# A residual kept in DRAM by plain copies, its squares and norm moved into the up projection

## The chip, the cores and the metric

One Trainium2 chip, one of its NeuronCores. The time is the device time of one execution of the whole program in microseconds (us); the shown time is the median of three runs. All data are float32. Matrix products run with operands split into two float32r parts, a high and a low one, three products for one.

## The reference

One decoder layer on x of 512 tokens by 2048 features. Only the end of it is touched:

```python
x = x + concat([attn, ssm]) @ w_out                # second residual
x = x + cross_attention(rms_norm(x, g_cross), ...) # third residual, ends with @ w_co
hm = rms_norm(x, g_mlp)                            # needs the sum of squares of each token
x = x + square(relu(hm @ w_up)) @ w_down           # w_up 2048x8192, w_down 8192x2048
```

The factor of `rms_norm` for one token, 1/sqrt(mean(x*x) + eps), is one number per token. It can be multiplied onto `hm @ w_up` behind the product, which is what the kernel does.

## The kernel before

Activations are held transposed: features on the 128 partitions, 512 tokens along the row. The residual is thus 16 blocks of 128x512 (256 KB each). Almost all scratch blocks come from one pool of 68 buffers of 128x512, `big()`; a new block waits until every reader of the old one is done, transfers included.

The cross-attention section runs from line 988 and is written under `manual_schedule`: on each engine its instructions keep the order in which they are written. Behind it the planner orders the instructions by their order in the text and by when it takes them to be ready. Instructions of the up projection may fall between those of the section.

The output product of the cross attention (lines 1053 to 1075) makes four groups of four feature blocks, n = 0 to 3. For each block `third_out` adds the second residual (`xr`, read from DRAM by `load_cols` on GpSimd's queue) to the PSUM bank, on VectorE, and scales it by g_mlp on ScalarE. `forms` makes from two such blocks the seven sums and differences that a Strassen-like 2x2 scheme with seven products needs, split in high and low parts (`XF`, which stays in 56 of the 68 buffers for the whole up projection). `third_keep(n)` then stores what is still needed of the third residual: it squares the four blocks on ScalarE and adds the squares into four DRAM tiles (`ss3d`, accumulating transfers on GpSimd's queue, a plain write for n = 0), and writes the halves of the blocks as initial values into the DRAM accumulators `accd` of the down projection (four plain pieces and one accumulating piece for two blocks). `clear()` has written zeros into the other pieces of `accd` much earlier, in 24 small transfers.

The up projection makes 32 pairs of column blocks, f = 0 to 31. Each has four quarters; a quarter is 42 matmuls of 256 columns (`up_products`, lines 946 to 948) on one weight tile of 512 KB, which SyncE's queue loads (line 913) and `up_forms` turns into forms: lines 926 and 931 on ScalarE (`rh`, `wh`), lines 927 to 930 and 932 on VectorE (`sw`, `rl`, `wl`). Weight tiles have four raw buffers, forms two sets. The seven products lie in four PSUM banks, which `combine` (lines 952 to 962) turns into two result blocks, and `up_finish` multiplies them with the token factor `rb`, takes relu and square, and writes them to DRAM on ScalarE's queue. The banks alternate between two sets of four, `mm` and `aux`.

f = 0 is computed inside the section (lines 1077 to 1088), f = 1 behind it. At the end of f = 1 `third_norm` (lines 974 to 986) reads the four `ss3d` tiles back on SyncE's queue, adds them on VectorE, sums over features with eight matmuls with a column of ones (line 261), makes 1/sqrt with six small instructions that alternate between VectorE and ScalarE (lines 175 to 180), and spreads the result over the partitions by four transposes on TensorE (line 984). Then f = 0 and f = 1 can be finished.

Of the kernel before, what the change touches and what calls it, by code (L numbers as in the profile page):

```python
# [9 lines left out]
F32 = mybir.dt.float32  # L10
F32R = mybir.dt.float32r
I32 = mybir.dt.int32
AF = mybir.ActivationFunctionType
OP = mybir.AluOpType
# [3 lines left out]
D = 2048  # L18
NT = 4
NK = 16  # L20
# [85 lines left out]
def tile_layer(ctx, tc, vec, xT, memT_d, pos, wqk, wv0, wv1, wv2, wzx, wout, wcq, wckv, wco, wup, wdn, out):  # L106
    nc = tc.nc
# [25 lines left out]
    def big(dtype=F32):  # L133
        return bp.tile([128, 512], dtype, name="b", tag="b")
# [4 lines left out]
    def small(w, name="s"):  # L139
        return sp.tile([128, w], F32, name=name, tag=f"s{w}", bufs=4 if w > 32 else 12)  # L140
# [31 lines left out]
    def rsqrt(dst, ssq, n):  # L172
        w = ssq.shape[1]
        v, y, t = small(w, "v"), small(w, "y"), small(w, "t")
        dve.tensor_scalar(v, ssq, 1.0 / n, EPS, op0=OP.mult, op1=OP.add)
        act.activation(y, v, AF.Ln)
        act.activation(y, y, AF.Exp, scale=-0.5)
        dve.tensor_tensor(t, y, y, OP.mult)
        dve.scalar_tensor_tensor(t, t, -0.5, v, op0=OP.mult, op1=OP.mult)
        dve.scalar_tensor_tensor(dst, t, 1.5, y, op0=OP.add, op1=OP.mult)  # L180
# [77 lines left out]
    def token_sums(sq, nt, tag="aux"):  # L258
        p, s = bank(tag), small(nt, "ts")
        for t in range(nt):  # L260
            pe.matmul(p[:, t:t + 1], sq[:, t * 128:t * 128 + 128], onec, start=True, stop=True)
        dve.tensor_copy(s, p[:, :nt])
        return s
# [605 lines left out]
    def third_out(n, xr, ps):  # L869
        xs = []  # L870
        for i in range(4):
            dve.tensor_tensor(xr[i], xr[i], ps[i], OP.add)
            xs.append(big())
            act.activation(xs[i], xr[i], AF.Copy, scale=c_mlp[:, 4 * n + i:4 * n + i + 1])
        return xs

    NJ = D // 256
    accd = [[dp.tile([128, 512 if b < 3 else 256], F32, name=f"acc{j}_{b}") for b in range(4)] for j in range(NJ)]  # L880
    ss3d = [dp.tile([128, 512], F32, name=f"ss{i}") for i in range(4)]

    def third_keep(n, xr):
        for i in range(4):
            q = big()
            act.activation(q, xr[i], AF.Square)
            if n:
                nc.gpsimd.dma_start(ss3d[i], q, accum_op=OP.add)
            else:
                nc.gpsimd.dma_start(ss3d[i], q)  # L890
        for i in range(2):
            xa, xb, b, m = xr[2 * i], xr[2 * i + 1], accd[2 * n + i], big()
            act.activation(m, xb, AF.Copy, scale=-1.0)
            nc.gpsimd.dma_start(b[1][:, H0], xa[:, H0])
            nc.gpsimd.dma_start(b[0][:, H1], xa[:, H1])
            nc.gpsimd.dma_start(b[3], m[:, H0])
            nc.gpsimd.dma_start(b[2][:, H1], m[:, H1])
            nc.gpsimd.dma_start(b[0][:, H1], xb[:, H1], accum_op=OP.add)

    def clear():  # L900
        z = big()
        nc.gpsimd.memset(z[:, H0], 0.0)
        for b in accd:
            for to in (b[0][:, H0], b[1][:, H1], b[2][:, H0]):
                nc.gpsimd.dma_start(to, z[:, H0])


    prods = ((4, 4, 0, H0), (5, 5, 1, H0), (6, 0, 3, H0), (2, 3, 2, H0), (3, 2, 2, H1), (1, 1, 1, H1), (0, 6, 0, H1))
# [2 lines left out]
    def up_weights(f, q, w=wup):  # L911
        raw = weight_tile["raw"]()
        nc.sync.dma_start(raw, w[f, q].rearrange("p a b c -> p (a b c)"))
        return raw
# [56 lines left out]
    def up_out(f, ps):  # L971
        up_finish(f, combine(ps, True))

    def third_norm():

        s4, r3 = [big() for _ in range(4)], small(4, "r3")
        for i in range(4):
            nc.sync.dma_start(s4[i], ss3d[i])
        for i in range(3):
            dve.tensor_tensor(s4[0], s4[0], s4[i + 1], OP.add)  # L980
        rsqrt(r3, token_sums(s4[0], NT, "mm"), D)
        p = bank("mm")
        for t in range(NT):
            pe.transpose(p[:, t * 128:t * 128 + 128], r3[:, t:t + 1].to_broadcast([128, 128]), ident)
        act.activation(rb[:, :512], p, AF.Copy)
        act.activation(rb[:, 512:], p[:, H0], AF.Copy)

    uw, uf = [], []
    with tc.manual_schedule():

        ps = [bank("mm") for _ in range(NT)]
        for k in range(8):
            take()
            mem_unit(k)
            take()
            if k == 4:
                rsqrt(r2, token_sums(acc2[0], NT), D)
            mms(ps, x2T, k, k, 8)

        psk = [bank() for _ in range(2)]  # L1000
        for k in range(8):
            take()
            if k == 0:
                dve.tensor_tensor(msq[0][:, H0], msq[0][:, H0], msq[0][:, H1], OP.add)
                qc = rows_out(ps, r2)
            if k == 1:
                sq = head_sums(qc)
            if k == 2:
                rq = head_rstd(sq)
            if k in (3, 4):  # L1010
                head_scale(qc, rq, (2 * k - 6, 2 * k - 5))
            if k == 5:
                mem_rstd()
            if k > 5:
                qcT += [head_T(qc, h, cqs) for h in (2 * k - 12, 2 * k - 11)]
            mms(psk, memT, 8 + k, k, 8)

        pend = []
        psv = [bank("mm") for _ in range(2)]
        for k in range(8):  # L1020
            take()
            if k == 0:
                kc = rows_out(psk, rm)
                sq = head_sums(kc)
            if k == 1:
                head_scale(kc, head_rstd(sq), range(2))
                xr = [load_cols(0)]
                clear()
            if k == 3:
                kcT += [head_T(kc, h, c_ck) for h in range(4)]  # L1030
            if k >= 4:
                for tp in range(2):
                    e = scores(k - 4, tp)
                    if pend:
                        normalize(*pend.pop())
                    pend.append(e)
            mms(psv, memT, 16 + k, k, 8)
        normalize(*pend.pop())
        vc = rows_out(psv, rm)
        pt = [probs_T(0), probs_T(1)]  # L1040
        OcT = []
        for h in range(4):
            OcT.append(weighted(h, pt[h], vc))
            if h < 2:
                pt.append(probs_T(h + 2))
        xr.append(load_cols(1))
        uw += [up_weights(0, 0), up_weights(0, 1), up_weights(0, 2)]

        def co(n, ps, k):
            for i in range(4):  # L1050
                mm3(ps[i], tuple(a[:, i * 128:i * 128 + 128] for a in cow[4 * n + k]), OcT[k], k == 0, k == 3)

        for n in range(4):
            ps = [bank("aux" if n % 2 else "mm") for _ in range(NT)]
            co(n, ps, 0)
            if n == 0:
                uf += [up_forms(w) for w in uw[:2]]
            if n in (1, 3):
                co(n, ps, 1)
            if n:  # L1060
                xc = xs
                hl = big(F32R), big(F32R)
                forms(xc[0], xc[1], hl, H0)
                third_keep(n - 1, xr[n - 1])
            if n in (1, 2):
                xr.append(load_cols(n + 1))
            if n in (0, 2):
                co(n, ps, 1)
            co(n, ps, 2)
            if n > 1:  # L1070
                forms(xc[2], xc[3], hl, H1)
            co(n, ps, 3)
            xs = third_out(n, xr[n], ps)
            if n == 1:
                forms(xc[2], xc[3], hl, H1)
        uw.append(up_weights(0, 3))
        pu = up_bank(0)
        up_products(pu, (0, 1), uf[0], XF, True, False)
        uf.append(up_forms(uw[2]))
        xc = xs  # L1080
        hl = big(F32R), big(F32R)
        forms(xc[0], xc[1], hl, H0)
        third_keep(3, xr[3])
        up_products(pu, (2, 3), uf[1], XF, False, False)
        uf.append(up_forms(uw[3]))
        forms(xc[2], xc[3], hl, H1)
        for q in (2, 3):
            up_products(pu, (2 * q, 2 * q + 1), uf[q], XF, False, q == 3)

    first_out = combine(pu, True)  # L1090


    NU = FF // 256

    def up_pairs(fs):
        for f in fs:
            ps = up_bank(f)
            for q in range(4):
                wf = up_forms(up_weights(f, q))
                up_products(ps, (2 * q, 2 * q + 1), wf, XF, q == 0, q == 3)  # L1100
            if f == 1:
                third_norm()
                up_finish(0, first_out)
            up_out(f, ps)

    up_pairs(range(1, NU - 4))

# [212 lines left out]
```

## Time and profile before

| | us |
|---|---|
| median of 3 runs (2328.46 to 2336.8) | 2331.66 |
| the profiled execution | 2326.44 |
| its span, first to last instruction | 2324.7 |
| TensorE busy | 2300.5 (99%) |
| VectorE busy | 1744.9 (75%) |
| ScalarE busy | 1186.8 (51%) |
| GpSimd busy | 203.9 (9%) |

Engines in the rows: PE is TensorE, PEld its weight loads, DVE VectorE, ACT ScalarE, POOL GpSimd, SP SyncE; a q behind the name is the engine's own queue. L888 is line 888. The granted clock (PEclk) is a share of full speed, 1.00 being 2.4 GHz and 0.50 being 1.2 GHz. Busy time is a union of intervals, so instructions that overlap by a pipeline's length count once. The cross-attention section's last part and the first pairs of the up projection lie between 970 and 1110 us of the span.

### The profile page before, as it was taken

How to read it: one execution, taken by the hardware profiler on the slowest of the kernel's cores; microseconds unless marked ns; L12 is line 12 of the kernel's file. 1: busy time of each engine (PE TensorE's matmuls, PEld its weight loads, DVE VectorE, ACT ScalarE, POOL GpSimd, SP SyncE). 2: the span in 40 equal slices, each digit the busy share in tenths (PEclk: the TensorE clock that was granted, in tenths of full speed). 3: DMA queues.
4: the chain of work that ended last, by engine and by line, in shares of the span. 5: the costliest groups of instructions: out<-in, count | busy, mean ns of one | idle time of the engine just before them, and what ended most of it. 6: DMA issues, size and time to landing. Idle time of an engine off the chain costs nothing.

```text
span 2324.7 us, 39884 instructions
## 1 busy us (share of the span) xinstructions
PE 2300.5 (99%) x15700; PEld 2107.1 (91%) x15700; DVE 1744.9 (75%) x2970; ACT 1186.8 (51%) x1845; POOL 203.9 (9%) x271
## 2 busy tenths in 40 slices
PE   9999999999999999999999999999999999999999
PEld 7889977777778888789999999999999999999999
DVE  7544277786674446688888888888998988888976
ACT  6335377655453336564444444444565555665653
POOL 0000000000000002150000000000032121332120
PEclk9999999999999999999999999999999999999999
DMA  5222311212224457384433334434597685987784
GB/s 201 86 93 76 103 64 55 64 64 82 74 74 156 140 180 255 124 195 153 136 128 132 128 132 137 133 131 136 164 245 186 170 204 161 225 206 181 220 213 171
DMA packets 129597, 335.74 MB, mean 144 GB/s; under 512 B 14848, under 2 KB 30336, under 8 KB 129408
## 3 DMA queue, kind: packets, MB, share of 16 engines
q1 hardware_dynamic: 82944, 256.61, 33.3%
q0 software_dynamic: 30848, 55.59, 13.1%
q10 hardware_dynamic: 15616, 20.98, 2.4%
q8 instruction: 123, 2.02, 0.3%
q14 instruction: 66, 0.54, 0.1%
HBM read 258.67 MB, written 74.45 MB: 143 GB/s over the span
## 4 chain that ended last, share of the span: by engine, by line
PE 92%; DMA 2%; DVE 2%; ACT 2%; issue 1%; POOL 1%; SPq 0%; DVEq 0%; POOLq 0%; ACTq 0%
PE mm L220 11%; PE mm L222 11%; PE mm L221 11%; PE mm L948 9%; PE mm L946 9%; PE mm L947 9%; PE aux L948 9%; PE aux L946 9%; PE aux L947 9%; DMA acc<-b 1%; PE aux L531 1%; PE aux L522 1%; PE aux L256 1%; PE aux L648 0%; PE aux L503 0%
## 5 line engine op out<-in xcount | busy, mean ns | idle before, releaser
L931 ACT ACTIVATE wh<-sw 128x1024 fp32r<-128x1024 f32 x253 | 268.1, 1060 | 380.1 <-PE mm L947 128.7
L932 DVE TENSOR_TENSOR wl<-sw,wh 128x1024 fp32r<-128x1024 f32 x253 | 308.8, 1221 | 124.9 <-ACT wh L931 124.5
L216 DVE TENSOR_TENSOR wl<-wr,wh 128x1024 fp32r<-128x1024 f32 (+2 forms) x143 | 166.6, 1165 | 193.9 <-ACT wh L215 193.3
L215 ACT ACTIVATE wh<-wr 128x1024 fp32r<-128x1024 f32 (+2 forms) x143 | 144.7, 1012 | 285.2 <-PE mm L222 151.4
L946 PE MATMUL mm<-b,wh 128*128 128x256 f32 x1024 | 288.8, 282 | 0.0
L948 PE MATMUL mm<-b,wl 128*128 128x256 f32 x1024 | 288.6, 282 | 0.0
L947 PE MATMUL mm<-b,wh 128*128 128x256 f32 x1024 | 287.7, 281 | 0.0
L946 PE MATMUL aux<-b,wh 128*128 128x256 f32 x1000 | 281.5, 282 | 0.0
L948 PE MATMUL aux<-b,wl 128*128 128x256 f32 x1000 | 281.0, 281 | 0.0
L947 PE MATMUL aux<-b,wh 128*128 128x256 f32 x1000 | 280.4, 280 | 0.0
L222 PE MATMUL mm<-b,wl 128*128 128x512 f32 x640 | 254.5, 398 | 1.1 <-DVE wl L216 1.1
L221 PE MATMUL mm<-b,wh 128*128 128x512 f32 x640 | 255.2, 399 | 0.0
L220 PE MATMUL mm<-b,wh 128*128 128x512 f32 x640 | 254.9, 399 | 0.1
L926 ACT ACTIVATE rh<-wr 128x768 fp32r<-128x768 f32 x190 | 161.4, 849 | 151.4 <-PE aux L947 56.7
L1193 POOL DMA_DIRECT2D acc<-b x160 | 139.8, 1324 | 1063.1 <-ACT b L1192 1062.0
L946 PE MATMUL mm<-b,rh 128*128 128x256 f32 x768 | 219.2, 285 | 4.7 <-ACT rh L926 4.3
L948 PE MATMUL mm<-b,rl 128*128 128x256 f32 x768 | 218.7, 285 | 1.0 <-DVE rl L930 1.0
L947 PE MATMUL mm<-b,rh 128*128 128x256 f32 x768 | 218.5, 285 | 0.0
L946 PE MATMUL aux<-b,rh 128*128 128x256 f32 x750 | 213.0, 284 | 0.0
L947 PE MATMUL aux<-b,rh 128*128 128x256 f32 x750 | 212.7, 284 | 0.0
L948 PE MATMUL aux<-b,rl 128*128 128x256 f32 x750 | 212.3, 284 | 0.0
L220 PE MATMUL mm<-wh,b 128*128 128x512 f32 (+2 forms) x544 | 201.6, 371 | 2.8 <-ACT b L430 1.6
(324 smaller groups left out, 5846.8 us busy)
## 6 DMA issues: line engine op xcount, KB each, us to landing
wr<-in_wup_dram SPq DMA_DIRECT2D x96, 512.0 KB, 3.4
wr<-in_wdn_dram SPq DMA_DIRECT2D x96, 512.0 KB, 4.6
acc<-b POOLq DMA_DIRECT2D x120, 256.0 KB, 6.6
wr<-in_wzx_dram SPq DMA_DIRECT2D x48, 512.0 KB, 3.3
zr<-in_wup_dram SPq DMA_DIRECT2D x32, 512.0 KB, 3.2
a<-b ACTq DMA_DIRECT2D x64, 256.0 KB, 2.2
b<-a SPq DMA_DIRECT2D x64, 256.0 KB, 5.7
zr<-in_wdn_dram SPq DMA_DIRECT2D x32, 512.0 KB, 3.9
```

What stands on the lines that cost most here:

```text
L215: act.activation(hi, raw, AF.Copy)
L216: dve.tensor_tensor(lo, raw, hi.bitcast(F32), OP.subtract)
L220: pe.matmul(ps, l[0], r[0], start=start, stop=False)
L221: pe.matmul(ps, l[0], r[1], start=False, stop=False)
L222: pe.matmul(ps, l[1], r[0], start=False, stop=stop)
L926: act.activation(rhi, q(raw, 0, 3), AF.Copy)
L931: act.activation(shi, sw, AF.Copy)
L932: dve.tensor_tensor(slo, sw, shi.bitcast(F32), OP.subtract)
L946: pe.matmul(ps[b][:, H], w[0][:, d], xf[0], start=st, stop=False, skip_group_check=True)
L947: pe.matmul(ps[b][:, H], w[0][:, d], xf[1], start=False, stop=False, skip_group_check=True)
L948: pe.matmul(ps[b][:, H], w[1][:, d], xf[0], start=False, stop=sp_, skip_group_check=True)
L1193: nc.gpsimd.dma_start(accd[j][b], o[:, w], accum_op=OP.add)
```

## The change

`third_out` writes each finished block of the third residual to a DRAM tile `x3d` by a plain transfer on ScalarE's queue. The squares and the initial values of the accumulators are no longer made in the section. In f = 1 and f = 2 of the up projection two blocks per quarter are read back on SyncE's queue, squared on ScalarE and added up on VectorE (`third_sum`). `third_norm` is split: the sum over features and the 1/sqrt come behind the first quarter of f = 3, the transposes (`third_rows`) behind its third, and there f = 0, 1 and 2, whose combined results are held till then, are finished. The calls of `third_keep` and `clear` in the section are gone; the five transfers of the old `third_keep` are those of the new one. In f = 4 to 11 one pair of blocks each is read back again, and `third_keep` writes its pieces, and the zeros of that pair, on GpSimd's queue.

```diff
             xs.append(big())
             act.activation(xs[i], xr[i], AF.Copy, scale=c_mlp[:, 4 * n + i:4 * n + i + 1])
+            act.dma_start(x3d[4 * n + i], xr[i])
         return xs
...
-    ss3d = [dp.tile([128, 512], F32, name=f"ss{i}") for i in range(4)]
-
-    def third_keep(n, xr):
-        for i in range(4):
-            q = big()
-            act.activation(q, xr[i], AF.Square)
-            if n:
-                nc.gpsimd.dma_start(ss3d[i], q, accum_op=OP.add)
-            else:
-                nc.gpsimd.dma_start(ss3d[i], q)
-        for i in range(2):
-            xa, xb, b, m = xr[2 * i], xr[2 * i + 1], accd[2 * n + i], big()
-            act.activation(m, xb, AF.Copy, scale=-1.0)
-            (five transfers on GpSimd's queue, as below)
-
-    def clear():
+    x3d = dp.tile([NK, 128, 512], F32, name="x3d")
+
+    def third_block(i):
+        b = big()
+        nc.sync.dma_start(b, x3d[i])
+        return b
+
+    def third_keep(j):
+        xa, xb, b, m = third_block(2 * j), third_block(2 * j + 1), accd[j], big()
+        act.activation(m, xb, AF.Copy, scale=-1.0)
+        nc.gpsimd.dma_start(b[1][:, H0], xa[:, H0])
+        nc.gpsimd.dma_start(b[0][:, H1], xa[:, H1])
+        nc.gpsimd.dma_start(b[3], m[:, H0])
+        nc.gpsimd.dma_start(b[2][:, H1], m[:, H1])
+        nc.gpsimd.dma_start(b[0][:, H1], xb[:, H1], accum_op=OP.add)
         z = big()
         nc.gpsimd.memset(z[:, H0], 0.0)
-        for b in accd:
-            for to in (b[0][:, H0], b[1][:, H1], b[2][:, H0]):
-                nc.gpsimd.dma_start(to, z[:, H0])
+        for to in (b[0][:, H0], b[1][:, H1], b[2][:, H0]):
+            nc.gpsimd.dma_start(to, z[:, H0])
+
+    acc3 = []
+
+    def third_sum(i):
+        b = third_block(i)
+        act.activation(b, b, AF.Square)
+        if i:
+            dve.tensor_tensor(acc3[0], acc3[0], b, OP.add)
+        else:
+            acc3.append(b)
...
+    r3 = cp.tile([128, 4], F32, name="r3")
+
     def third_norm():
-        s4, r3 = [big() for _ in range(4)], small(4, "r3")
-        for i in range(4):
-            nc.sync.dma_start(s4[i], ss3d[i])
-        for i in range(3):
-            dve.tensor_tensor(s4[0], s4[0], s4[i + 1], OP.add)
-        rsqrt(r3, token_sums(s4[0], NT, "mm"), D)
+        rsqrt(r3, token_sums(acc3[0], NT, "mm"), D)
+
+    def third_rows():
         p = bank("mm")
         for t in range(NT):
             pe.transpose(p[:, t * 128:t * 128 + 128], r3[:, t:t + 1].to_broadcast([128, 128]), ident)
...
-    first_out = combine(pu, True)
     NU = FF // 256
+    held = [combine(pu, True)]
 
     def up_pairs(fs):
         for f in fs:
             ps = up_bank(f)
             for q in range(4):
                 wf = up_forms(up_weights(f, q))
+                if f in (1, 2):
+                    for i in range(2):
+                        third_sum(8 * f - 8 + 2 * q + i)
                 up_products(ps, (2 * q, 2 * q + 1), wf, XF, q == 0, q == 3)
-            if f == 1:
-                third_norm()
-                up_finish(0, first_out)
-            up_out(f, ps)
+                if f == 3 and q == 0:
+                    third_norm()
+                if f == 3 and q == 2:
+                    third_rows()
+                    for i in range(3):
+                        up_finish(i, held[i])
+                if 4 <= f < 4 + NJ and q == 1:
+                    third_keep(f - 4)
+            if f < 3:
+                held.append(combine(ps, True))
+            else:
+                up_out(f, ps)
```

## Rows read from the trace of the kernel before

**Rows 1.** The page: the whole span, busy us of each engine.
```profile
PE 2300.5 (99%) x15700; PEld 2107.1 (91%) x15700; DVE 1744.9 (75%) x2970; ACT 1186.8 (51%) x1845; POOL 203.9 (9%) x271
```
**Rows 2.** Windows: busy us by engine, then granted clock, DMA share, GB/s.
```profile
core 0: us, PE busy (x) PEld busy (x) DVE busy (x) ACT busy (x) POOL busy (x), PEclk, DMA share, GB/s
970.00:1010.88 40.88, 40.88 (x183) 33.84 (x181) 32.08 (x61) 28.43 (x51) 18.40 (x31) 1.00 0.57 151
1010.88:1060.81 49.93, 44.69 (x340) 43.45 (x338) 41.45 (x72) 26.93 (x42) 23.21 (x35) 0.93 0.84 216
1060.81:1090.55 29.74, 24.96 (x189) 24.87 (x189) 22.35 (x41) 12.52 (x18) 0.00 (x0) 0.89 0.38 125
1090.55:1110.55 20.00, 20.00 (x171) 20.00 (x170) 17.22 (x27) 8.96 (x12) 0.00 (x0) 1.00 0.41 134
```
**Rows 3.** Timeline of TensorE: start, us, instruction, idle before and releaser.
```profile
1010.88 0.28 PE L946 MATMUL mm<-b,rh 128*128 128x256 f32 x1
...
1022.36 0.38 PE L946 MATMUL mm<-b,rh 128*128 128x256 f32 x1 [1.32 <-ACT rh L926]
...
1032.84 0.39 PE L946 MATMUL mm<-b,rh 128*128 128x256 f32 x1 [2.94 <-ACT rh L926]
...
1060.61 0.95 PE L261 MATMUL mm<-onec,b 128*128 128x1 f32 x8
1066.34 1.12 PE L984 MATMUL mm<-cst,r 128*128 128x128 f32 x4 [4.78 <-DVE r L180]
...
1067.47 0.41 PE L947 MATMUL mm<-b,rh 128*128 128x256 f32 x1
```
**Rows 4.** Timeline of ScalarE in the second wait.
```profile
1030.51 0.63 ACT L893 ACTIVATE b<-b 128x512 f32<-128x512 f32 x1 [1.49 <-DMA acc<-b]
...
1031.96 0.83 ACT L926 ACTIVATE rh<-zr 128x768 fp32r<-128x768 f32 x1
```
**Rows 5.** Timeline of GpSimd: two transfers of the keeping, the last loads of xr.
```profile
1008.66 0.89 POOL L898 DMA_DIRECT2D acc<-b x1 [5.28 <-DVE b L712]
1013.59 2.52 POOL L866 DMA_DIRECT2D b<-x2d x4
```
**Rows 6.** Timeline of VectorE.
```profile
1016.08 0.69 DVE L195 TENSOR_TENSOR b<-b 128x512 fp32r<-128x512 f32 x1 [1.63 <-DMA acc<-b]
1017.68 2.00 DVE L872 TENSOR_TENSOR b<-b,aux 128x512 f32<-128x512 f32 x3 [0.90 <-DMA b<-x2d]
1024.66 0.42 DVE L852 TENSOR_TENSOR b<-b 128x256 f32<-128x256 f32 x1
1026.46 1.89 DVE L195 TENSOR_TENSOR b<-b 128x512 fp32r<-128x512 f32 x3
1054.21 0.69 DVE L980 TENSOR_TENSOR b<-b 128x512 f32<-128x512 f32 x1 [1.33 <-DMA b<-ss]
```
**Rows 7.** Page, DMA issues: count, KB each, median us to landing.
```profile
x2d<-b ACTq DMA_DIRECT2D x16, 256.0 KB, 2.0
ss<-b POOLq DMA_DIRECT2D x16, 256.0 KB, 7.5
b<-ss SPq DMA_DIRECT2D x4, 256.0 KB, 4.4
```
**Rows 8.** Groups of ScalarE, 975 to 1036 us: busy us, mean ns, idle before.
```profile
L886 ACT ACTIVATE b<-b 128x512 f32<-128x512 f32 x16 | 8.7, 616 | 0.0
L893 ACT ACTIVATE b<-b 128x512 f32<-128x512 f32 x8 | 4.7, 619 | 1.8 <-DMA acc<-b 1.8
```
**Rows 9.** ScalarE's queue, line 686: its 16 issues, ns min/median/max.
```profile
L686 ACTq DMA_DIRECT2D x2d<-b x16: 326/326/344, 708.2 to 856.7; - x16
```
**Rows 10.** Groups of VectorE, 1140 to 1300 us (eight pairs f).
```profile
L932 DVE TENSOR_TENSOR wl<-sw,wh 128x1024 fp32r<-128x1024 f32 x32 | 39.1, 1221 | 20.6 <-ACT wh L931 20.6
L967 DVE SCALAR_TENSOR_TENSOR b<-b,rb 128x512 f32<-128x512 f32 x16 | 10.3, 681 | 0.0
```
**Rows 11.** Waits of SyncE's queue, 1080 to 1300 us: total, times, longest.
```profile
SPq L913 <- DVE sw L929: 105.6, 22, 5.4
```

More of the change, by code (lines that the diff above doesn't have):

```diff
@@ L880, in tile_layer @@
     accd = [[dp.tile([128, 512 if b < 3 else 256], F32, name=f"acc{j}_{b}") for b in range(4)] for j in range(NJ)]
-    ss3d = [dp.tile([128, 512], F32, name=f"ss{i}") for i in range(4)]
-    def third_keep(n, xr):
-        for i in range(4):
-            q = big()
-            act.activation(q, xr[i], AF.Square)
-            if n:
-                nc.gpsimd.dma_start(ss3d[i], q, accum_op=OP.add)
-            else:
-                nc.gpsimd.dma_start(ss3d[i], q)
-        for i in range(2):
-            xa, xb, b, m = xr[2 * i], xr[2 * i + 1], accd[2 * n + i], big()
-            act.activation(m, xb, AF.Copy, scale=-1.0)
[L894 to L898, printed above, removed]
-    def clear():
+    x3d = dp.tile([NK, 128, 512], F32, name="x3d")
[11 more added lines that the diff above has]
+        nc.gpsimd.dma_start(b[0][:, H1], xb[:, H1], accum_op=OP.add)
         z = big()
         nc.gpsimd.memset(z[:, H0], 0.0)
-        for b in accd:
-            for to in (b[0][:, H0], b[1][:, H1], b[2][:, H0]):
-                nc.gpsimd.dma_start(to, z[:, H0])
+        for to in (b[0][:, H0], b[1][:, H1], b[2][:, H0]):
[8 more added lines that the diff above has]
+            acc3.append(b)
     prods = ((4, 4, 0, H0), (5, 5, 1, H0), (6, 0, 3, H0), (2, 3, 2, H0), (3, 2, 2, H1), (1, 1, 1, H1), (0, 6, 0, H1))
@@ L1027, in tile_layer @@
                 xr = [load_cols(0)]
-                clear()
             if k == 3:
@@ L1063, in tile_layer @@
                 forms(xc[0], xc[1], hl, H0)
-                third_keep(n - 1, xr[n - 1])
             if n in (1, 2):
@@ L1082, in tile_layer @@
         forms(xc[0], xc[1], hl, H0)
-        third_keep(3, xr[3])
         up_products(pu, (2, 3), uf[1], XF, False, False)
```

## The prediction

> **What bounds the kernel now.** I read the page's busy times first, then windows over the up projection, then TensorE's timeline and, back from each of its waits, the engine that ended it. The page shows TensorE busy for 99% of the span [rows 1]: only stretches where it waits, or runs at half clock, can be won. The windows say where. From 1090.55 on, one pair f takes 20.00 us with TensorE busy throughout at a granted clock of 1.00. The three pairs before it (f = 0 to 2) take 49.93 + 29.74 = 79.67 us where three such pairs take 60.00. The loss is 19.7 us, all of it beside the code that the change touches [rows 2]. In the stretch ahead, 970 to 1010.88, TensorE is busy for all 40.88 us [rows 2], so nothing can be won there.
>
> The loss has two halves. Between 1010.88 and 1060.81 it is 49.93 - 40.00 = 9.9 us: 5.2 us idle (49.93 - 44.69), the rest mostly half clock after the waits (mean granted clock 0.93) [rows 2]. The two longest waits are 1.32 and 2.94 us, both for ScalarE's `rh` [rows 3]. Behind the second stands a ScalarE that cannot go on: line 893, the negated copy of `third_keep`, waits 1.49 us for a buffer that a transfer into `accd` still reads, and `rh` is queued behind it [rows 4]. GpSimd's queue is late in the same way: its accumulating piece waits 5.28 us (for the plain piece that it adds to, by the code), and the loads of `xr` for n = 3 come out only at 1013.59, behind it [rows 5]. VectorE, in turn, waits for such a buffer (1.63 us) and for `xr` (0.90 us), and starts the last `third_out` at 1017.68, though TensorE had the banks ready by 1010.88 [rows 3, 6]. Between 1060.81 and 1090.55 the loss is 29.74 - 20.00 = 9.7 us [rows 2]: 4.78 us waiting for r3, then `rb`'s transposes, and matmuls at a duration of 0.41 instead of 0.28 us, at half clock [rows 3].
>
> **The change part by part.** All times stand against the profiled execution (2326.44 us, span 2324.7, so 1.7 us around it); it lies 5.2 us under the median shown, and I carry the difference over to that.
>
> (a) The section. ScalarE loses 16 squares and 8 copies, 8.7 + 4.7 = 13.4 us [rows 8], and gets 16 issues of 0.326 us [rows 9], 5.2 us. GpSimd's queue keeps only the loads of `xr`, so these are issued as soon as four buffers are free. The buffers of a block come free after one plain write, whose kin landed in 2.0 us, not after squares and a chain of accumulating transfers, which landed in 7.5 us [rows 7]. The Trainium skill ("DMA: Bandwidth & Descriptors", "Latency and other measured facts") gives about 0.6 us to the first byte of a transfer of SyncE's or ScalarE's queue and about 1 us for GpSimd's; going by those 0.4 us alone the buffers would hardly come sooner and (a) would keep nearly all of its 9.9 us. The rows disagree: 5.5 us apart, the accumulation and the queue ahead of it included.
>
> What is late next in f = 0 is VectorE. From 1010 on it owes four adds of `third_out`, two `up_forms` and two `forms`. The adds come at 2.00 us for three, 2.7 for four; one `forms` went from 1024.66 to 1028.35, 3.7 us [rows 6]; one `up_forms` is at most (17.22 - 1.29) / 4 = 4.0 us, a quarter of a steady pair without its finishing [rows 2, 10], combine counted in. Together 2.7 + 8.0 + 7.4 = 18.1, done at 1028. TensorE wants the second `forms` in its last quarter, from 1010.88 + 15 + 1, about 1027. So I leave 1.0 us in f = 0 and 1 (bounds 0 and the 9.9 of now, if the buffers stay as short).
>
> (b) `third_norm`. It waits for nothing new: eight small matmuls (0.95 us) and the step from the transposes to the next matmuls (1067.47 - 1066.34 = 1.1 us, at half clock [rows 3]) stay. The chain to r3 took 1066.34 - 1060.61 - 0.95 = 4.8 us; between the two parts now lie two quarters, 10 us of matmuls. I leave 1.5 us (bounds 0.9, and 6.3 if the chain is still late by all its 4.8 us).
>
> (c) VectorE in f = 1 to 3. It has 17.22 us of work in a pair of 20.00 [rows 2]. f = 1 gets 7 additions and f = 2 eight, 0.69 us each [rows 6] or, pipelined as in line 872's row, about 0.61; both lose their finishing, 10.3 / 8 = 1.29 us [rows 10]. f = 3 gets three finishings and r3's small steps, about 0.5. So 17.2 + 4.3 - 1.3 = 20.2, 17.2 + 4.9 - 1.3 = 20.8, 17.2 + 3.9 + 0.5 = 21.6: 62.6 against 60.0, or 63.8 at 0.69 each. VectorE becomes the bound by 2.6 to 3.8 us. It has a lead in steady pairs (its waits, 20.6 us in eight, are for ScalarE's `wh` [rows 10], which by the code waits for a free set of forms), but f = 0 ends without one. I take 3.5 us (bounds 1 and 10: the same share of waiting as in steady pairs, 20.6 / 8 x 3 = 7.7, on top of the 2.6).
>
> (d) What hides the rest. ScalarE's 16 squares of 0.62 us lie in pairs where it works 8.96 of 20 us [rows 2, 8]. SyncE's 32 reads share the queue of the weight tiles; this queue waits mostly for a raw tile to come free (105.6 us in 220) [rows 11], so it has the time, and with four tiles a load stands some three quarters, 15 us, ahead of its use. If a read waits for a buffer at the head of that queue, the weights behind it wait too; 15 us is the cover. From f = 4 on GpSimd has 8 transfers and a fill per pair, idle before [rows 2]; no engine waits for them until the down projection, so 0 (bounds 0 and 3 us, for a DMA share rising from 0.41; at 0.84 in f = 0 and 1 [rows 2] I see it cost only through buffers). The clearing in the section goes at no gain, since TensorE has no wait there that it made.
>
> Sum: of 19.7 us lost, 1.0 + 1.5 + 3.5 + 0 = 6.0 stay. The gain is 13.7 us: 2326.4 - 13.7 = 2312.7 for a run like the profiled one, 2331.7 - 13.7 = 2318.0 for the median.
>
> **Rivals.** (A) VectorE bounds f = 1 to 3 by its upper end, 10 us, and the waits bring 2 us more of half clock, as each of the two waits now does (9.9 - 5.2 = 4.7 for two). Then 1.0 + 1.5 + 12 = 14.5 stay, 5.2 are won: 2326.5. For it: 62.6 us of work in 60. Against it: at most 3.8 over by the sum.
> (B) The buffers stay short in the section, because SyncE's first reads for f = 1 fall into it and take four, and the splits of `forms` wait as now. (a) keeps 8.5: 8.5 + 1.5 + 3.5 = 13.5 stay, 6.2 won: 2325.5. Against it: six transient buffers per group are gone. The rule of the Trainium skill that (a) cites would end here too, since the buffers would come no sooner.
> (C) Slower: the read, the square and the addition of a block are not run ahead, and VectorE, in order, stands at each addition for its block. Line 980 stood 1.33 us for its read [rows 6]; with the square's 0.62 behind it that is 1.95 us, 15 times, 29.3 us, with nothing free on VectorE to take it up. 1.0 + 1.5 + 2.6 + 29.3 = 34.4 stay, 14.7 us slower than now: 2346.4. It decides from (19.7 - 5.1) / 15 = 1.0 us per addition. Against it: a read lands in 4.4 us [rows 7], and the queue issues it with weight tiles that stand 15 us ahead.
> (D) The change does what it says, but r3 is late at the transposes by all of 4.8 us: 10.8 stay, 8.9 won, 2322.8, within the forecast's own range.
>
> **How the numbers follow.** Forecast (with D) 0.63, own range 2312 to 2324; A 0.16, B 0.10, C 0.11. About 0.3%, 7.0 us, is what a measurement can tell from no change. Faster (under 2324.7) takes 0.61 of the forecast and a third of A and B, 0.09: 0.70. Slower (over 2338.7) is C less its milder half-cases plus little: 0.10. The same: 0.20. The range 2311 to 2329 leaves out C and some 0.07 of the tails, since A and B end at 2326.5 and runs of the kernel before lie 3 to 5 us apart.
>
> **What would show it.** Right: no wait of ScalarE for a transfer between 1010 and 1040; `xr` for n = 3 read well before 1010; f = 0 ending near 1032; no wait of TensorE over 1 us at the transposes; pair f = 4 ending 13 to 14 us sooner than now; from then on 20.00 us per pair. For A: VectorE busy over 9.5 of 10 in f = 1 to 3 and many short waits of TensorE for `rl` and `wl`. For B: lines 194 or 711 of ScalarE waiting for a transfer or for TensorE. For C: waits of VectorE in `third_sum` for ScalarE or a read. I am wrong if any pair after f = 4 takes longer than 20.00 us, or if the stretch before 1010.88 grows.

## The result, and the profile after

| us | before | after |
|---|---|---|
| median (runs) | 2327.3 (6, three of them those shown before) | 2317.66 (6) |
| lowest to highest | 2325.58 to 2336.8 | 2310.84 to 2320.4 |
| the profiled execution | 2326.44 | 2317.23 |
| its span | 2324.7 | 2314.9 |

The ratio of the means is 0.9947, with a 95% interval from 0.9924 to 0.997: 12.3 us less, between 7.0 and 17.7. The medians lie 9.6 us apart. The change is faster by more than the 0.3%, 7.0 us, that a measurement can tell from nothing, though the interval ends just there. The median came within 0.4 us of the forecast of 2318.0, but partly by luck: the starting point, 2331.7, was 4.4 us above the median of six runs, and the stretch that the change touches won more than forecast.

The page of the changed kernel, busy us by engine, shows what [rows 1] shows: TensorE is still the bound, with next to the same work.

```profile
PE 2299.7 (99%) x15700; PEld 2105.7 (91%) x15700; DVE 1749.3 (76%) x2982; ACT 1187.8 (51%) x1845; POOL 193.1 (8%) x262
```

Spans of single executions mix the change with differences that it didn't make (last section). So I measure the stretch itself, in every kernel in the same way: from the first matmul of f = 0 to ScalarE's first copy of `combine` for f = 5, less six pairs of 20.00 us. I call this the loss over six pairs. Before it is 1150.55 - 1010.88 - 120.00 = 19.67 us, the loss that the prediction started from. After it is 1139.92 - 1016.20 - 120.00 = 3.72 us. So 15.95 us were won, where 13.7 were forecast. Two windows, before and then after, hold the same 1031 matmuls between these marks (so do all the kernels below), and the granted clock stands behind their busy time:

```profile
1010.88:1150.55 139.67, 129.65 (x1031) 128.32 (x1030) 115.45 (x192) 66.35 (x92) 23.21 (x35) 0.95 0.56 161
...
1016.20:1139.92 123.72, 123.39 (x1031) 122.82 (x1030) 116.50 (x197) 68.99 (x98) 9.98 (x18) 1.00 0.58 189
```

Six pairs have 6 x 168 = 1008 and the norm 12, so 11 matmuls, 1.3 us at 20.00/168 us each, lie behind the six pairs in every kernel. They are in the 19.67 and in the 3.72 alike: they don't touch a difference, but 1.3 us of either is no loss. These are the instructions that begin and end the measure in the kernel after, on TensorE and on ScalarE (start, us, instruction); the third row is the copy one pair later, 20.00 us on.

```profile
1016.20 0.28 PE L951 MATMUL mm<-b,rh 128*128 128x256 f32 x1
...
1139.92 0.36 ACT L960 ACTIVATE b<-aux 128x256 f32<-128x256 f32 x1
...
1159.92 0.36 ACT L960 ACTIVATE b<-mm 128x256 f32<-128x256 f32 x1
```

Windows of the kernel after over the same work as [rows 2] (busy us by engine, granted clock, DMA share, GB/s): four stretches of 20 us from the first matmul of f = 0, and one steady pair that also holds a `third_keep`.

```profile
1016.20:1036.20 20.00, 19.81 (x166) 19.60 (x164) 18.18 (x34) 11.64 (x18) 0.00 (x0) 1.00 0.37 127
1036.20:1056.20 20.00, 20.00 (x169) 19.84 (x168) 19.20 (x33) 13.08 (x19) 0.00 (x0) 1.00 0.58 193
1056.20:1076.20 20.00, 19.86 (x167) 19.65 (x166) 20.00 (x33) 11.01 (x16) 0.00 (x0) 1.00 0.63 208
1076.20:1096.20 20.00, 20.00 (x171) 20.00 (x170) 18.87 (x35) 9.34 (x14) 0.00 (x0) 1.00 0.39 126
1139.92:1159.92 20.00, 20.00 (x171) 20.00 (x170) 17.14 (x27) 9.65 (x14) 5.00 (x9) 1.00 0.66 210
```

The granted clock is 1.00 throughout, where it was 0.93 and 0.89; GpSimd is silent in the four stretches; the DMA share is 0.37 and 0.58 in the first two, where it was 0.84. VectorE is busy for all 20.00 us of the third stretch. The waits of TensorE from 1010 to 1140 us (total, times, longest) are one row, in place of the 1.32, 2.94 and 4.78 us of [rows 3]:

```profile
PE aux L953 <- DVE rl L935: 0.2, 1, 0.2
```

Five rows say why. GpSimd issues the loads of `xr` for n = 3 from 991.96 on, 24 us ahead of f = 0, where [rows 5] had 1013.59, 2.7 us behind it. VectorE starts the last `third_out` 0.5 us before f = 0, where [rows 6] had 6.8 us behind it. And between sums and transposes of the norm TensorE now works.

```profile
991.96 1.06 POOL L866 DMA_DIRECT2D b<-x2d  x2 [18.66 <-PE aux L222]
994.68 1.06 POOL L866 DMA_DIRECT2D b<-x2d  x2 [1.66 <-PE aux L222]
...
1015.70 2.47 DVE L872 TENSOR_TENSOR b<-b,aux 128x512 f32<-128x512 f32 x4
...
1082.41 0.95 PE L261 MATMUL mm<-onec,b 128*128 128x1 f32 x8
...
1093.36 0.60 PE L989 MATMUL mm<-cst,r 128*128 128x128 f32 x4
```

### The profile page after: what moved, and what is told of

It reads as the page before. It is cut to its first block, busy times and chain, and to the rows that moved or that the text cites. A ratio compares the mean times of both kernels' runs of the same rounds, so it can differ in the third digit from the quotient of the medians.

```text
span 2314.9 us, 39983 instructions
## 1 busy us (share of the span) xinstructions
PE 2299.7 (99%) x15700; PEld 2105.7 (91%) x15700; DVE 1749.3 (76%) x2982; ACT 1187.8 (51%) x1845; POOL 193.1 (8%) x262
## 4 chain that ended last, share of the span: by engine, by line
PE 72%; issue 18%; POOL 5%; DVE 2%; ACT 1%; DMA 1%; SPq 0%; POOLq 0%; DVEq 0%; ACTq 0%
PE mm L220 11%; PE mm L222 11%; PE mm L221 11%; PE mm L953 5%; PE mm L951 5%; PE mm L952 5%; PE aux L953 5%; PE aux L951 5%; PE aux L952 5%; POOL acc L1205 5%; PE aux L531 1%; PE aux L522 1%; PE aux L256 1%; DMA wr<-in_wqk_dram 1%; PE aux L221 1%
```

## The experiments

Each kernel ran once, beside the kernel before on the same chip; the loss over six pairs, from its trace, tells more than the total. "Section" is the loss to ScalarE's first copy of `combine` for f = 1, less 40.00 us, with which the norm has nothing to do. That mark does not stand behind the same work everywhere: 339 to 342 matmuls lie ahead of it, but 347 in e1 and e3 and 356 in e7. At 0.119 us a matmul, 340 matmuls for all would make it 9.9 us in e1, 0.6 in e3 and 0.9 in e7.

| kernel | built on | loss, six pairs | section | us | kernel before beside it |
|---|---|---|---|---|---|
| before | | 19.67 | 9.93 | 2326.44 | |
| after | | 3.72 | 0.89 | 2317.23 | |
| e1_norm_late | before | 12.39 | 10.77 | 2322.21 | 2327.22 |
| e2_norm_in_one | after | 3.73 | 0.89 | 2312.99 | 2327.22 |
| e3_squares_early | after | 3.05 | 1.43 | 2316.53 | 2327.22 |
| e4_pieces_early | after | 3.74 | 0.88 | 2312.59 | 2327.22 |
| e6_loads_sync | before | 19.49 | 9.88 | 2331.09 | 2332.26 |
| e5_after_66 | after | 3.39 | 0.98 | 2314.80 | 2332.26 |
| e8_three_adds | after | 23.45 | 0.88 | 2333.74 | 2332.26 |
| e11_norm_aux | before | 15.12 | 10.18 | 2329.44 | 2332.26 |
| e13_scalar_only | after | 4.69 | 1.92 | 2312.52 | 2331.83 |
| e14_last_keep_later | before | 19.65 | 9.40 | 2332.60 | 2331.83 |
| e15_later_and_sync | before | 17.48 | 7.82 | 2324.90 | 2331.83 |
| e7_one_buffer | after | 25.64 | 2.82 | 2340.33 | 2331.83 |

**e1_norm_late**: the kernel before, with its norm alone moved as in the kernel after.

```diff
+                if f == 3 and q == 0:
+                    third_norm()
+                if f == 3 and q == 2:
+                    third_rows()
+                    for i in range(3):
+                        up_finish(i, held[i])
```

> The kernel before with one part of the change alone: the norm is split and moved to pair f = 3 (sum behind its first quarter, transposes behind its third), f = 0 to 2 are held; squares and initial values stay in the section. The measure is the loss over the first six pairs: from the first matmul of f = 0 to ScalarE's first copy of combine for f = 5, less 6 x 20.00 us. It is 19.7 us before and 3.7 us after. Theory (two separate halves): the 9.9 us of the section stay, the 9.7 us of the norm shrink to 1.5 to 2, so 11 to 12.5 us. Rival (one chain: the late section is also what makes r3 late, and with the norm moved VectorE catches up by itself): 5 to 8 us. Rival (the reads of the four square tiles wait for the accumulating transfers wherever they stand): above 15 us.

The loss is 12.39 us, as the first theory said. The section's half stays (10.77, or 9.9 over as many matmuls as before), the norm's half is gone but for 12.39 - 10.77 = 1.6. TensorE's waits in this kernel are the two for `rh` and two short ones for `rl`; none is at the transposes:

```profile
PE mm L946 <- ACT rh L926: 5.3, 2, 4.2
PE mm L948 <- DVE rl L930: 0.7, 2, 0.5
```

So the two halves are separate, and add up: the late norm is worth 19.67 - 12.39 = 7.3 us, the rest of the change 12.39 - 3.72 = 8.7.

**e2_norm_in_one**: the kernel after, the norm in one piece behind the third quarter of f = 3.

```diff
-                if f == 3 and q == 0:
+                if f == 3 and q == 2:
                     third_norm()
-                if f == 3 and q == 2:
                     third_rows()
```

> The changed kernel with the norm in one piece: sum, 1/sqrt and transposes all behind the third quarter of f = 3. Theory (TensorE stands in order at the transposes for the whole chain to r3, which took 4.8 us before, and runs at half clock for some us after): the loss over the first six pairs rises from 3.7 to 9 to 12 us, with one wait of TensorE of 4 to 5 us. Rival (the chain was long only because the kernel before had VectorE late): a wait of 1 to 2 us, loss 5 to 6 us.

Nothing came back: 3.73, below what either theory or rival expected. The distance of two quarters is not what saves the norm. TensorE's timeline in this kernel shows it: the transposes follow 4.5 us behind the sums, where it was 5.7 us before, a chain not much shorter; but 0.81 us behind the first of the sums matmuls of the next quarter run, into `aux` banks.

```profile
1089.35 0.95 PE L261 MATMUL mm<-onec,b 128*128 128x1 f32 x8
1090.16 0.36 PE L951 MATMUL aux<-b,rh 128*128 128x256 f32 x1
...
1093.82 0.60 PE L989 MATMUL mm<-cst,r 128*128 128x128 f32 x4
```

Why TensorE stood in the kernel before, then, is the next question, and **e11_norm_aux** asks it: at the end of f = 1 the norm took two banks of the `mm` set, and by the code the next pair, f = 2, needs all four. Here it takes them from `aux`.

```diff
-        rsqrt(r3, token_sums(s4[0], NT, "mm"), D)
-        p = bank("mm")
+        rsqrt(r3, token_sums(s4[0], NT), D)
+        p = bank()
```

> The kernel before with one word changed: the two PSUM banks of the norm at the end of f = 1 come from the aux set instead of the mm set. The run with the norm in one piece showed no wait of TensorE, since matmuls of the same pair went between the sums and the transposes. Theory (before, TensorE had nothing to put between them, because the next pair needs all four mm banks of which the norm held two): with the norm in aux banks matmuls of f = 2 go between, the wait of 4.78 us goes, and the loss over the first six pairs falls from 19.7 to 11 to 13 us. Rival (the wait stands wherever the norm's banks are, since the order of TensorE's instructions follows the text): it stays at 18 to 20 us.

The mechanism holds, its size does not. Matmuls of f = 2 come between sums and transposes, and the wait of 4.78 us is gone. A wait of 0.93 us ahead of the sums is left; what ends it is `combine` of f = 1 (L957), which still reads an `aux` bank:

```profile
1065.68 1.05 PE L261 MATMUL aux<-onec,b 128*128 128x1 f32 x8 [0.93 <-DVE b L957]
1066.60 0.36 PE L946 MATMUL mm<-b,rh 128*128 128x256 f32 x1
...
1067.67 0.41 PE L947 MATMUL mm<-b,wh 128*128 128x256 f32 x1
...
1071.64 0.60 PE L984 MATMUL aux<-cst,r 128*128 128x128 f32 x4
```

Yet only 19.67 - 15.12 = 4.5 us are won; 15.12 - 10.18 = 4.9 stay behind the section, where e1 has 1.6 over eight matmuls fewer. The third row shows a part of it: matmuls of 0.41 in place of 0.28 us, half clock again. This kernel's window shows a granted clock of 0.83 for these 10 us:

```profile
1063.35:1073.35 10.00, 9.07 (x64) 0.83 0.25 90
```

**e3_squares_early** and **e4_pieces_early** divide the section's half: the kernel after, with either the squares (with their accumulating transfers) or the pieces and zeros of `accd` put back into the section.

```diff
+                third_squares(n - 1, xr[n - 1])   # e3: 4 squares, each added into ss3d
...
+                third_pieces(n - 1, xr[n - 1])    # e4: 2 x 5 transfers into accd, from SBUF
```

> The changed kernel, but the squares are made in the section and added into four DRAM tiles by accumulating transfers as before (the norm reads them back in f = 3); the initial values stay late, from read-back blocks. Theory (the initial values were the larger cause, since ScalarE stood at their negated copy): loss over the first six pairs 5 to 8 us. Rival (the accumulating transfers of the squares, 1.7 us each of GpSimd's queue against 0.9 to 1.1 for the others, hold the queue and the buffers): 10 to 12 us, as in the run with the norm alone moved.

> The changed kernel, but the initial values and the zeros are written in the section as before, from the blocks in SBUF; the squares stay late, from read-back blocks. Theory (the initial values were the larger cause): loss over the first six pairs 8 to 11 us, with ScalarE waiting at the negated copy. Rival (the squares were the cause): 4 to 6 us, no wait of ScalarE for a transfer.

All four theories and rivals missed: neither is the cause by itself, with 1.43 (0.6 over as many matmuls) and 0.88 us in the section. Only both together cost 10.77 (e1; 9.9). The windows over f = 0 and 1 of the two kernels, first e3, then e4, show GpSimd at 3.72 and 10.00 us and TensorE with next to no gap; before, GpSimd had 23.21 us in 50 [rows 2].

```profile
1012.97:1052.97 40.00, 39.89 (x335) 39.68 (x334) 38.52 (x67) 23.22 (x33) 3.72 (x5) 1.00 0.65 170
```

```profile
1010.88:1050.88 40.00, 39.81 (x332) 39.46 (x331) 38.77 (x68) 25.77 (x38) 10.00 (x16) 1.00 0.71 221
```

The loads of `xr` for n = 3 are issued 12.0 us (e3) and 7.4 us (e4) before f = 0 begins; with both halves in the section 2.7 us (before) or 1.9 us (e1) behind it.

**e6_loads_sync, e14_last_keep_later, e15_later_and_sync**: three tries at the kernel before that take away one consequence each, the last one two: the loads of `xr` on SyncE's queue, past GpSimd's backlog; the last `third_keep` behind the `forms` of the fourth quarter, so that no `rh` is queued behind it; both.

```diff
-            nc.gpsimd.dma_start(xr[i], x2d[4 * n + i])
+            nc.sync.dma_start(xr[i], x2d[4 * n + i])      # e6, e15
...
-        third_keep(3, xr[3])
         up_products(pu, (2, 3), uf[1], XF, False, False)
...
         forms(xc[2], xc[3], hl, H1)
+        third_keep(3, xr[3])                              # e14, e15
```

> The kernel before, but the second residual's blocks (load_cols) are read on SyncE's queue instead of GpSimd's; squares, initial values and norm are as before. Measured so far, loss over the first six pairs: before 19.7, after 3.7; with the squares alone left in the section 3.1, with the initial values alone 3.7, with both and the norm moved 12.4. So the two parts cost nothing each and some 9 us together. The loads of xr for n = 3 went out late with both (2 us into f = 0), 9 to 12 us ahead of f = 0 with one of them, 18 to 22 us ahead with none. Theory (the two fill GpSimd's queue together, and the loads behind them come late): with the loads off that queue the section's loss of 9.9 us falls to 1 to 4 us, the total to 11 to 14 us; no wait of VectorE for xr. Rival (buffers: the two together use the last ones, and the loads and the splits wait for those): the loss stays at 17 to 20 us.

> The kernel before with one line moved: the keeping of the last group (third_keep(3)) is written behind the forms of the fourth quarter of f = 0 instead of ahead of them. Nothing is left out. Theory (ScalarE, in order, stands in that call for buffers and the rh behind it comes late): the wait of 2.94 us and the half clock behind it go, the first wait (1.32 us) stays: the section's loss falls from 9.9 to 4 to 6 us, the total from 19.7 to 14 to 16. Rival (the buffers are short wherever the call stands, and the splits of forms wait for them instead): the section's loss stays at 8 to 10 us.

> The kernel before with both: the last keeping moved behind the forms of the fourth quarter, and the loads of xr on SyncE's queue. With the loads alone moved the first wait went, but the second grew from 2.94 to 6.6 us, ScalarE standing 2.40 us for a transfer of the squares and 2.19 for one into accd. Theory (two causes in series: xr late behind GpSimd's queue, then ScalarE standing in the last keeping): the section's loss falls from 9.9 to 0.5 to 2.5 us, the total to 10 to 12.5 us. Rival (something else in the section, or the half clock, remains): the section's loss stays above 4 us.

All three theories fell, and the rivals held: 9.88, 9.40 and 7.82 us stay in the section. Each time the wait came back elsewhere. In e6 ScalarE stands at the squares and the negated copies, for buffers that GpSimd's transfers still read, and `rh` is queued behind them; TensorE waits 6.6 us for it. ScalarE's timeline in e6:

```profile
1029.06 1.91 ACT L886 ACTIVATE b<-b 128x512 f32<-128x512 f32 x3 [2.40 <-DMA ss<-b]
1031.16 0.63 ACT L886 ACTIVATE b<-b 128x512 f32<-128x512 f32 x1 [0.18 <-DMA acc<-b]
1033.98 0.63 ACT L893 ACTIVATE b<-b 128x512 f32<-128x512 f32 x1 [2.19 <-DMA acc<-b]
1034.88 0.63 ACT L893 ACTIVATE b<-b 128x512 f32<-128x512 f32 x1 [0.27 <-DMA acc<-b]
1035.42 0.83 ACT L926 ACTIVATE rh<-zr 128x768 fp32r<-128x768 f32 x1
```

In e14 TensorE waits for VectorE's `rl` instead; in e15 VectorE itself stands, in the subtractions of `forms`, for a buffer that a transfer reads. One row of the waits of each, e14 first:

```profile
PE mm L948 <- DVE rl L930: 2.5, 2, 2.0
```

```profile
DVE b L195 <- DMA acc<-b: 2.3, 1, 2.3
```

**e13_scalar_only** asks whether ScalarE's time matters: the kernel after, with 24 squares into buffers that nothing reads.

```diff
+    def extra(xr):
+        for i in range(6):
+            q = big()
+            act.activation(q, xr[i % 4], AF.Square)
...
+                extra(xr[n - 1])
```

> The changed kernel with ScalarE's work of the old keeping put back where it stood, and nothing else of it: six squares per group of four blocks, 24 in all, 0.62 us each, into buffers that no one reads (no transfers). Loss over the first six pairs so far: before 19.7, after 3.7; with GpSimd's queue freed of the loads of xr still 19.5, with two buffers fewer than after 3.4. Theory (ScalarE stands for buffers that GpSimd's transfers still read; its own time is not the cause): loss 3 to 5.5 us. Rival (ScalarE's 13 to 15 us of extra work in the section, in order ahead of the rh of the fourth quarter, is the cause): 8 to 12 us.

It hardly does, as the theory said: the loss is 4.69, and the section goes from 0.89 to 1.92, 1.0 us for 24 squares of some 0.62 us each.

**e5_after_66** asks whether the kernel after is short of buffers: `NBUF` 66 for 68.

> The changed kernel with 66 instead of 68 buffers of 128x512. Theory (GpSimd's queue, not the number of buffers, made the section late): loss over the first six pairs below 6 us. Rival (buffers): with two fewer the section waits again, for a transfer or for TensorE's last read of a buffer: 7 to 12 us.

It is not: 3.39. The opposite test, more buffers for the kernel before, was not tried.

**e8_three_adds** asks how near VectorE is to its bound: every addition of `third_sum` three times (which also changes the sum).

```diff
-            dve.tensor_tensor(acc3[0], acc3[0], b, OP.add)
+            for _ in range(ADDS):
+                dve.tensor_tensor(acc3[0], acc3[0], b, OP.add)
...
+ADDS = 3
```

> The changed kernel with each addition of squares made three times (the output differs by that): 30 more instructions of 0.61 us on VectorE in f = 1 and 2, 18.3 us. VectorE was busy 18.2, 19.2, 20.0 and 18.9 of 20 us in the first four pairs, so it has 3.7 us free there. Theory (VectorE is at its bound there, the forecast's step c): the loss over the first six pairs rises from 3.7 by what doesn't fit, to 14 to 19 us. Rival (VectorE has a lead and slack that busy shares don't show): below 9 us.

The loss, 23.45, is above the 14 to 19 us expected. It rises by 19.7 us, for 30 further additions of 0.61 us, 18.3: as much as all of it comes through, and the granted clock falls to 0.91 and 0.83 in two stretches. The 3.7 us that VectorE had free in the first four stretches took up nothing. The windows of this kernel show VectorE busy without a gap in the first two and TensorE at some 16 of 20 us:

```profile
1050.00:1070.00 20.00, 15.76 (x120) 15.55 (x119) 20.00 (x35) 9.83 (x15) 0.00 (x0) 0.91 0.43 132
1070.00:1090.00 20.00, 16.22 (x129) 15.38 (x127) 20.00 (x33) 6.66 (x9) 0.00 (x0) 1.00 0.29 107
1090.00:1110.00 20.00, 16.24 (x121) 16.24 (x122) 18.98 (x36) 7.34 (x12) 0.00 (x0) 0.83 0.23 79
```

**e7_one_buffer** builds rival C: after the first blocks all reads go into one buffer, so that a block can't be read ahead.

```diff
+        if i > 1:
+            b = one[0]
+            nc.sync.dma_start(b, x3d[i])
...
```

> The changed kernel with the blocks 1 to 15 of the sum of squares read into one and the same buffer, so that each read waits for the addition of the block before it and none runs ahead. After, the reads went out in two bursts of eight, and no engine waited over 2.7 us for one. Theory (rival C of the forecast, read 4.4 + square 0.62 + addition 0.69 = 5.7 us in series, on the queue of the weight tiles): 15 x 5.7 = 86 us for what f = 1 and 2 have 40 us for; less the 15 us that the weights stand ahead, the loss over the first six pairs rises from 3.7 to 25 to 40 us. Rival (the weights in the same queue and the sum overlap better than that, since only the norm in f = 3 waits for the sum): below 12 us.

The loss is 25.64 us, at the lower end of what was expected, and 8.5 us are lost against the kernel before beside it; rival C had 34.4 and 14.7. The way is another one too: f = 1 and 2 run nearly undisturbed (2.51 behind f = 2), though VectorE stands 10.9 us in all for squares; the sum is late, and TensorE stands 18.4 us in f = 3 for it. TensorE's and ScalarE's longest waits in this kernel:

```profile
PE mm L261 <- DVE b L913: 18.4, 1, 18.4
...
ACT b L911 <- DMA b<-x3d: 26.0, 12, 4.0
```

So without reading ahead the change loses. The kernel after reads in two bursts of eight (the x8 in the timeline of SyncE's queue, first), and its ScalarE waits for a read once, for 2.7 us (the row of its waits, second), while TensorE goes on.

```profile
1042.38 5.01 SPq L886 DMA_DIRECT2D b<-x3d  x8
1055.39 8.87 SPq L886 DMA_DIRECT2D b<-x3d  x8
```

```profile
ACT b L906 <- DMA b<-x3d: 2.7, 1, 2.7
```

By the total, no kernel of these beats the kernel after by more than its executions differ. By the loss, e3 is 0.67 us lower (3.05 against 3.72), in one execution each; after, e2 and e4 agree within 0.02.

## Why the prediction was right, point by point

The two halves of the loss, and the code that each belongs to, were read rightly: e1 parts them.

(a), 1.0 us to stay in the section: 0.89. The reason was half right. Buffers held by GpSimd's transfers and the late `xr` are what goes. But I put it down to the squares and the pieces alike, and to the landing of the squares, 7.5 us against 2.0 [rows 7]. Each alone costs next to nothing (e3, e4), though in e3 the squares still land a median 6.3 us behind their issue; only both together cost. For a transfer's first byte the Trainium skill ("DMA: Bandwidth & Descriptors", "Latency and other measured facts") gives about 0.6 us on SyncE's or ScalarE's queue and about 1 us on GpSimd's. By these 0.4 us alone rival B would have come, as the prediction said; the 0.89 us that stayed in the section disagree.

How the two work together can be read from the trace of the kernel before, ahead of the wait in [rows 4]. These are rows of GpSimd's timeline there:

```profile
1015.73 3.95 POOL L888 DMA_DIRECT2D ss<-b  x4
...
1018.75 2.05 POOL L895 DMA_DIRECT2D acc<-b  x1
...
1027.43 0.89 POOL L898 DMA_DIRECT2D acc<-b  x1 [5.58 <-DVE b L195]
```

The plain piece (L895), issued behind four accumulating squares, lands 8.2 us after its issue, at 1026.9. The accumulating piece (L898), which by the code adds to it, goes out 0.5 us behind that, after a wait of 5.58 us (the row's releaser had long been done), and holds GpSimd's queue till then. It lands 3.0 us later, at 1030.5; that is the transfer that ScalarE's line 893 waits for at 1030.51, with `rh` behind it. The same wait is 5.28 us at 1008.66, ahead of the loads of `xr` [rows 5]. Where no squares go out just ahead of the two pieces it is 1.32 or 1.39 us. In e3 no piece waits in this queue, in e4 no squares delay one (the longest wait there, 5.23 us, comes behind the loads of `xr`). But this is read from a trace: no run wrote the pieces ahead of the squares, and none parts this from the load on the DMA engines (a share of 0.84 before, 0.71 in e4, 0.65 in e3). e6, e14 and e15 took away single waits behind it, and the wait moved.

(b), 1.5 us for the norm: 1.6 in e1 (12.39 - 10.77) and in e3 (3.05 - 1.43), where the additions don't blur it and 347 matmuls lie ahead of the first mark in both. The reason given was wrong: two quarters between sums and transposes are not needed (e2). What the move does is to put the norm where TensorE has matmuls that need none of the norm's banks. In the kernel before it had none, since f = 2 needed the banks that the norm held (e11).

(c), 3.5 us for VectorE in f = 1 to 3: mis-sized, it was some 0.3. Behind the section 3.72 - 0.89 = 2.8 us are counted; 0.95 of them are the eight matmuls that lie behind the first mark here and ahead of it in e1 and e3, and 1.6 are the norm. The price of an addition, 0.61 to 0.69 us, was right (line 872's row in [rows 6] gives 0.66 in a series, though, not 0.61); this row of VectorE in the kernel after, 1016 to 1097 us, is their group (busy us, mean ns, idle before):

```profile
L908 DVE TENSOR_TENSOR b<-b 128x512 f32<-128x512 f32 x15 | 10.2, 681 | 0.0
```

What failed is that the sum took f = 1 to 3 by themselves, with all three finishings in f = 3, and every us over 60.0 as a loss. VectorE had room around the full third stretch: 19.20 us of work in the second and 18.87 in the fourth; and it was busy for 18.98 and 18.87 us in the two stretches behind these four, where a later pair takes 17.14, so that work went on there. TensorE waited 0.2 us. e8 shows that there was no more room: 18.3 us of further additions come through in full. So rival A did not come; how few us more on VectorE would have brought it was not tried.

(d), 0 for the rest: right in the up projection. A pair with its `third_keep` takes 20.00 us, at a DMA share of 0.66.

The sum: 3.7 us stay where 6.0 were forecast, by (c); of the 19.7 that it starts from, 1.3 us are matmuls and no loss. Of what would show it, two statements failed. "f = 0 ending near 1032" (some 21 us behind its first matmul): its first `combine` copy came 26.2 us behind, since TensorE did matmuls of f = 1 first; the loss behind f = 1 shows that this cost nothing. And pair f = 4 was to end 13 to 14 us sooner: by the time of the trace it was 1139.92 against 1150.55 one pair later, 10.6, because f = 0 began 5.3 us later in this execution. (From f = 4 to f = 5 the copies of the kernel after lie 20.90 us apart, but over seven matmuls more than in a steady pair, 178 against 171 in their windows; TensorE is busy throughout, at a clock of 1.00.) "The stretch before 1010.88 grows" was to prove me wrong, and it grew; by the last section that is not the change.

## What to carry to other kernels

Side work that holds buffers by slow transfers is priced by what stands in order behind the buffers. Here the price was no sum of its parts: either half was all but free where both cost 9 us, and moving one consequence only moved the wait. Look for a transfer that waits, in an ordered queue, for the landing of another behind slow ones. A short serial chain costs the bound engine nothing where that engine has other work that needs none of the chain's banks; look at what it may do meanwhile, before at the distance. And work handed to a nearly full engine cost 0.3 us as long as later work could slide into the next pairs, and all of its time once the engine was full: add up the whole stretch over which work may slide, not each pair.

## What the runs showed of the hardware

The same instructions took a different time in different executions, far ahead of the change. f = 0 began at 1010.88 us before and at 1016.20 after. Some 3 us of this were there within the first 100 us of the span. Another part lies at 695 to 705 us, where TensorE's windows (busy us, granted clock, DMA share, GB/s) show half the stretch and more at 1.2 GHz after, and none before; before first, then after, then e6, which is built on the kernel before, then e4, built on the kernel after:

```profile
695.00:705.00 10.00, 10.00 (x44) 1.00 0.52 177
```

```profile
695.00:705.00 10.00, 9.40 (x27) 0.66 0.33 105
```

```profile
695.00:705.00 10.00, 9.79 (x33) 0.74 0.33 105
```

```profile
695.00:705.00 10.00, 10.00 (x45) 1.00 0.56 173
```

Both clocks occur with both kernels. f = 0 began at 1009.86 to 1014.50 us in the kernels built on the kernel before, at 1010.79 to 1016.20 in those built on the kernel after. So some five us ahead of a change of sixteen are not its doing: the totals of these two executions differ by 9.2 us. A stretch between two marks of the trace shows the change itself.

The clock fell in e11 behind a wait of 0.93 us and eight small matmuls, and in the kernel before behind waits of 1.32 and 2.94; in the kernel after, eight such matmuls without a wait left it at 1.00.

ScalarE's last copy of `combine`, at the end of the up projection, came 10.62 us sooner after than before (1660.17 against 1670.79), the end of the span 9.8: some 0.8 us was given back in the down projection, which I did not trace further.
